# Gate tables from three bf16 products with the token as the last index, and value products in pairs of units

## The chip, the cores and the metric

The kernel runs on one core of a Trainium2 chip. The metric is the device time of one execution in microseconds; lower is better. TensorE (PE in the profile; PEld is its weight load), VectorE (DVE), ScalarE (ACT), GpSimd (POOL) and the DMA queue of SyncE (SP) work side by side and wait for one another through semaphores.

## What is computed

The reference chains two transformer blocks over 512 tokens of width 1024. The last part of the second block is a PEER feed-forward layer. For each token and each of 8 heads it picks 16 of 128 x 128 experts, and uses them with softmax weights:

```python
experts = jnp.take_along_axis(cand_i, best_pos, axis=-1)
g = jax.nn.softmax(best_s, axis=-1)
act = jax.nn.gelu(jnp.einsum('thkd,td->thk', expert_u[experts], xb).astype(jnp.float32))
wgt = (g * act).astype(xb.dtype)
return jnp.einsum('thk,thkd->td', wgt, expert_v[experts])
```

All inputs and the output are float32. The first block's second layer is a forgetting attention with 16 heads (8 pairs) over 4 query tiles of 128 tokens.

## The kernel before

The work is one long program of stages: even mixer, feed-forward, odd mixer (`odd`), feed-forward, the second block's mixer (`second`), and `peer`. Big products are made in three float32r matmuls of split operands (`mm3`, L181 to L183). Each engine runs its instructions in a fixed order.

**Gate tables in `peer`.** For the first 384 tokens (three tiles of 128) the kernel doesn't gather experts: it multiplies all 16384 experts densely and weighs them with a table G of 128 x 128 gates for each token. A token has 128 picks (8 heads x 16), which lie on the partitions: `idx[0]` and `idx[1]` hold the two index halves of each pick, `idx[2]` its gate. `flush` (L1582) turns a tile's three fields to that layout with PE transposes and ACT copies (L1588). `peer_pair` (L1652) then makes, for a block of `TB` = 16 tokens, two one-hot tables `oB` and `Ag` of 128 picks x (16 tokens x 128 keys) in float32, by two `is_equal` on DVE (L1659); it multiplies `Ag` with the gate, 8 tokens in one DVE instruction (L1662) and 8 tokens each in an ACT instruction (L1664). `peer_g` (L1667) makes one float32 matmul for each token, `oB[:, token]` as weights and `Ag[:, token]` as moving operand (L1675), four tokens into a PSUM bank; ACT copies the bank to `st` with the token as last index (L1676), and SP writes `st` to `Gd` in DRAM (L1677).

The order is written out in the loop over the 24 blocks: `peer_g` of a block, `peer_pair` of the next, then one `u_block` (two in every third turn), then two indirect gathers of experts for the last tile of tokens, which GpSimd issues and DVE uses. A `u_block` is 24 float32r matmuls of 128 x 384 (L181 to L183) on a panel of `peer_u`, which is loaded by SP, split by ACT (L170) and DVE (L175). There are 24 + 8 = 32 of them in this loop.

**Attention in `odd`.** `attend` (L501) runs over 32 units, a pair of heads p and a query tile i in order. In step u it issues some matmuls of projection panels, the scores of unit u (L480, L481, L1036) with their softmax on DVE and ACT, the value products of unit u-2 (L1046), and the transposes of unit u-1 (L496 in `p_t`), whose results go to buffers `PT`, three of them. A value product has 64 columns of weights and writes one half of the PSUM partitions, so the two heads of a pair stand side by side in the array.

Of the kernel before, what the change touches and what calls it, by code (L numbers as in the profile page):

```python
# [10 lines left out]
F32 = mybir.dt.float32  # L11
F32R = mybir.dt.float32r
BF16 = mybir.dt.bfloat16
U32 = mybir.dt.uint32
I32 = mybir.dt.int32
AF = mybir.ActivationFunctionType
ALU = mybir.AluOpType
# [4 lines left out]
P = 128  # L22
D = 1024
T = 512
# [9 lines left out]
NKEY = 128  # L34
TB = 16
TD = T - P
# [14 lines left out]
class Builder:  # L51
    def __init__(self, nc, tc, ctx, ins, out, plan=None):
        self.nc, self.tc, self.ctx, self.I, self.out = nc, tc, ctx, ins, out
        ec = ctx.enter_context
        self.cp = ec(tc.tile_pool(name="cp", bufs=1))
        self.wp = ec(tc.tile_pool(name="wp", bufs=4))
        self.big = ec(tc.tile_pool(name="big", bufs=3))
        self.np_ = ec(tc.tile_pool(name="np", bufs=2))
        self.flip = 0
        self.qs_bufs = 3  # L60
        self.lo_pool = False
        self.nx = self.nst = self.last_evac = None
        self.npre = 0
        self.log, self.plan, self.pos, self.ready, self.look = [], plan, 0, [], 2
        self.x = self.cp.tile([P, NT, D], F32, name="x")
        for t in range(NT):
            nc.sync.dma_start(self.x[:, t], ins["x"][t * P:(t + 1) * P])
        self.idn = self.cp.tile([P, P], F32, name="idn")
        nc.sync.dma_start(self.idn, ins["idn"])
        self.idb = self.cp.tile([P, P], BF16, name="idb")  # L70
        nc.vector.tensor_copy(self.idb, self.idn)
        self.gcols = self.cp.tile([P, 6, KD], F32, name="gcols")
        nc.sync.dma_start(self.gcols, ins["gcols"])
        self.ones = self.cp.tile([P, P], F32, name="ones")
        nc.vector.memset(self.ones, 1.0)
        self.adacol = self.cp.tile([P, 6, KD], F32, name="adacol")
        self.adabc = self.cp.tile([P, 6, KD], F32, name="adabc")
        nc.sync.dma_start(self.adabc, ins["adab_col"])
        self.sc = self.cp.tile([P, 2, KD], F32, name="sc")
        nc.sync.dma_start(self.sc, ins["cc"])  # L80
# [408 lines left out]
            nc.vector.tensor_mul(rs, rs, gate)  # L489
        nc.vector.tensor_scalar(Pm[:, :n], Pm[:, :n], rs, None, op0=ALU.mult)  # L490

    def p_t(self, wk, Pm, nb, tag="PT", bufs=3):
        nc = self.nc
        tp = self.tt_()
        for b in range(nb):
            nc.tensor.transpose(tp[:, b * P:(b + 1) * P], Pm[:, b * P:(b + 1) * P], self.idn)  # L496
        PT = wk.tile([P, T], F32, name=tag, tag=tag, bufs=bufs)
        self.copy(PT[:, :nb * P], tp[:, :nb * P])
        return PT

    def attend(self, wk, units, score, nb, value, panels, want, finish):  # L501


        done, Pm, PT = 0, {}, {}
        left = {}
        for u in units:
            left[u[0]] = left.get(u[0], 0) + 1
        for u in range(len(units) + 2):
            for _ in range(want(u) - done):
                next(panels, None)  # L510
                done += 1
            if u < len(units):
                sms = [wk.tile([P, 1], F32, name="sm", bufs=6) for _ in range(2)]
                Pm[u] = [score(*units[u], e, sms[e]) for e in range(2)]
                for e in range(2):
                    self.norm_p(wk, Pm[u][e], nb(units[u][1]) * P, sms[e])
            if u >= 2:
                p = units[u - 2][0]
                value(*units[u - 2], PT.pop(u - 2))
                left[p] -= 1  # L520
                if left[p] == 0:
                    finish(p)
            if 0 <= u - 1 < len(units):
                PT[u - 1] = [self.p_t(wk, q, nb(units[u - 1][1])) for q in Pm.pop(u - 1)]
        for _ in panels:
            pass
# [421 lines left out]

    def odd(self):
        nc, tc, I = self.nc, self.tc, self.I  # L950
        self.qs_bufs = 2
        h = self.norm_t()
        with ExitStack() as cx:
            ap = cx.enter_context(tc.tile_pool(name="odp", bufs=1))
            wk = cx.enter_context(tc.tile_pool(name="odw", bufs=2))
# [7 lines left out]
            of = self.big.tile([P, KD, T], F32, name="of", tag="big")  # L963
# [12 lines left out]
            ps = self.ot_()  # L976
# [22 lines left out]
                nc.sync.dma_start(c6, I["one6"][0:1].broadcast_to([P, 8 * T]))  # L999
                nc.sync.dma_start(c6[0:3] if q else c6[3:6], I["one6"][1:2].broadcast_to([3, 8 * T]))  # L1000
            for i in range(3):
                pc = wk.tile([P, T], BF16, name="pc", tag="PT", bufs=3)[0:16]
                nc.vector.tensor_copy(pc, cum)
                if i < 2:
                    nc.vector.tensor_sub(cum, cum, pc)
                ng = wk.tile([P, T], BF16, name="ng", tag="PT", bufs=3)[0:16]
                nc.vector.tensor_scalar(ng, pc, -1.0, None, op0=ALU.mult)
                nc.sync.dma_start(cd[0, i], pc)
                nc.sync.dma_start(cd[1, i], ng)
# [3 lines left out]
            QK, po = {}, {}  # L1013
# [37 lines left out]
            def fill():  # L1051
# [3 lines left out]
                for k in range(6):  # L1055
# [4 lines left out]
            units = [(p, i) for p in range(8) for i in range(NT)]  # L1060
            self.attend(wk, units, score, lambda i: i + 1, value, fill(),
                        lambda u: min(128, 4 * u + 20) + max(0, 2 * u - 56),
                        lambda p: self.copy(of[:, p], po[p]))
            self.sqrt_table(self.last_exp)
            self.split_k(oT, of, (6, 7))
            w3 = ap.tile([P, 4, D], F32R, name="w3", tag="cq6", bufs=1)
# [75 lines left out]
    def second(self):  # L1142
        nc, tc, I = self.nc, self.tc, self.I
        self.qs_bufs = 2
        with ExitStack() as c0:
            p0 = c0.enter_context(tc.tile_pool(name="s2p", bufs=1))
            uT = p0.tile([P, 4, T], F32, name="uT", tag="uT", bufs=1)
            h = self.norm_t()
            with ExitStack() as cx:
                ap = cx.enter_context(tc.tile_pool(name="s2a", bufs=1))  # L1150
                dp = cx.enter_context(tc.tile_pool(name="s2d", bufs=1, space=DRAM))
                wk = cx.enter_context(tc.tile_pool(name="s2w", bufs=2))
# [11 lines left out]
                for q in range(2):  # L1164
                    ps = self.mmt()
# [22 lines left out]
            with ExitStack() as cx:  # L1188
                ap = cx.enter_context(tc.tile_pool(name="s2g", bufs=1))
                wk = cx.enter_context(tc.tile_pool(name="s2n", bufs=2))  # L1190
# [24 lines left out]
                for c in range(4):  # L1215
                    ps = self.ot_()
# [100 lines left out]
    def peer(self):  # L1317
        nc, tc, I = self.nc, self.tc, self.I
        self.look = 0
        with ExitStack() as c0:  # L1320
# [16 lines left out]
                nc.scalar.copy(h2t[:, c * T:(c + 1) * T], tp)  # L1337
            gk = ExitStack()
            ep = gk.enter_context(tc.tile_pool(name="pee", bufs=2))
            idx = [ep.tile([P, TD], F32, name=f"ix{q}", bufs=1) for q in range(3)]  # L1340
            it128 = ep.tile([P, NKEY], F32, name="it128", bufs=1)
            nc.sync.dma_start(it128, I["iota"].broadcast_to([P, NKEY]))
            eid = ap.tile([P, P], I32, name="eid")
            g3 = ap.tile([P, P], F32, name="g3")
            act3 = ap.tile([P, P], F32, name="act3")
# [79 lines left out]
                        next(gs)  # L1425
                        ng -= 1
            gp = gk.enter_context(tc.tile_pool(name="peg", bufs=2))
            behind[0], pair = self.peer_pair(gp, idx, it128, 0)
            for tb in range(NTB):
                self.peer_g(gp, pair, tb, Gd)  # L1430
                if tb + 1 < NTB:
                    behind[0], pair = self.peer_pair(gp, idx, it128, tb + 1)
                if tb == 4:
                    next(steps, None)
                u_block()
                if tb % 3 == 2:
                    u_block()
                for _ in range(2 if tb < NTB - GSTOP else 0):
                    next(gs, None)
# [102 lines left out]
    def peer_topk(self, wk, h, idx, it128, eid, g3, ep):  # L1542
# [39 lines left out]
        def flush():  # L1582
            t, ef = wait
            tp = self.tt_()
            for q in range(3):
                nc.tensor.transpose(tp[:, q * P:(q + 1) * P], ef[q], self.idn)
            for q in range(3):
                nc.scalar.copy(idx[q][:, t * P:(t + 1) * P], tp[:, q * P:(q + 1) * P])  # L1588

        for t in (3, 0, 1, 2):  # L1590
            c = wk.tile([P, 8, NC_], F32, name="cand")
# [60 lines left out]
    def peer_pair(self, wk, idx, it, tb):  # L1652

        nc = self.nc
        ia, ib, g = [q[:, tb * TB:(tb + 1) * TB] for q in idx]
        oB = wk.tile([P, TB, NKEY], F32, name="oB")
        Ag = wk.tile([P, TB, NKEY], F32, name="Ag")
        for o, ix in ((oB, ib), (Ag, ia)):
            nc.vector.tensor_tensor(o, it.unsqueeze(1).broadcast_to([P, TB, NKEY]),  # L1659
                                    ix.unsqueeze(2).broadcast_to([P, TB, NKEY]), op=ALU.is_equal)  # L1660
        n = TB // 2
        last = nc.vector.tensor_tensor(Ag[:, 0:n], Ag[:, 0:n], g[:, 0:n].unsqueeze(2).broadcast_to([P, n, NKEY]), op=ALU.mult)  # L1662
        for t in range(n, TB):
            nc.scalar.activation(Ag[:, t], Ag[:, t], AF.Copy, scale=g[:, t:t + 1])  # L1664
        return last, (oB, Ag)

    def peer_g(self, wk, pair, tb, Gd):  # L1667

        nc = self.nc
        oB, Ag = pair  # L1670
        st = wk.tile([P, NKEY, TB], F32, name="gst")
        for q in range(TB // 4):
            ps = self.tt_() if q % 2 else self.st_()
            for t in range(4):
                nc.tensor.matmul(ps[:, t * P:(t + 1) * P], oB[:, q * 4 + t], Ag[:, q * 4 + t], start=True, stop=True)  # L1675
            nc.scalar.copy(st[:, :, q * 4:q * 4 + 4].rearrange("p i t -> p t i"), ps.rearrange("p (t i) -> p t i", t=4))  # L1676
        nc.sync.dma_start(Gd[tb], st)  # L1677

# [181 lines left out]
```

## Time and profile before

| | us |
|---|---|
| median of 3 runs | 3028.69 (3024.31 to 3030.38) |
| profiled execution, its own time | 3035.33 |
| span of the profiled execution | 3033.6 |
| PE busy | 2983.7 (98%) |
| DVE busy | 2153.1 (71%) |
| ACT busy | 1394.7 (46%) |
| stretch of the gate tables, about 1990 to 2215 | 225 |
| stretch of the attention in `odd`, about 812 to 984 | 172 |

Matmuls are pipelined and the ends of their records are modelled, so PE's cost is read from the distances between starts in the timeline, not from the durations. Lines are those of the kernel before.

### The profile page before, as it was taken

How to read it: one execution, taken by the hardware profiler on the slowest of the kernel's cores; microseconds unless marked ns; L12 is line 12 of the kernel's file. 1: busy time of each engine (PE TensorE's matmuls, PEld its weight loads, DVE VectorE, ACT ScalarE, POOL GpSimd, SP SyncE). 2: the span in 40 equal slices, each digit the busy share in tenths (PEclk: the TensorE clock that was granted, in tenths of full speed). 3: DMA queues.
4: the chain of work that ended last, by engine and by line, in shares of the span. 5: the costliest groups of instructions: out<-in, count | busy, mean ns of one | idle time of the engine just before them, and what ended most of it. 6: DMA issues, size and time to landing. Idle time of an engine off the chain costs nothing.

```text
span 3033.6 us, 42326 instructions
## 1 busy us (share of the span) xinstructions
PE 2983.7 (98%) x15672; PEld 2526.6 (83%) x15672; DVE 2153.1 (71%) x3994; ACT 1394.7 (46%) x2374; POOL 638.3 (21%) x661
## 2 busy tenths in 40 slices
PE   8999999999999999999999999999999999999998
PEld 6867787788777878888888889999988888888887
DVE  3378798745577655556853689979947777777777
ACT  4466532224455443445662344568743333333333
POOL 2400000000000000000000100146625555555451
PEclk9999999999999999999999999999999999999999
DMA  4210367624311355554332326889899989999884
GB/s 130 84 36 22 95 192 223 193 83 135 101 49 41 118 182 193 193 188 140 104 98 91 110 79 200 282 297 323 309 319 309 339 310 337 311 331 319 316 307 162
DMA packets 212262, 580.19 MB, mean 191 GB/s; under 512 B 19372, under 2 KB 86092, under 8 KB 208588
## 3 DMA queue, kind: packets, MB, share of 16 engines
q1 hardware_dynamic: 167128, 414.95, 41.3%
q0 software_dynamic: 44352, 161.50, 14.8%
q8 instruction: 123, 2.02, 0.3%
q10 hardware_dynamic: 576, 1.05, 0.1%
q14 instruction: 83, 0.68, 0.1%
HBM read 522.80 MB, written 54.62 MB: 190 GB/s over the span
## 4 chain that ended last, share of the span: by engine, by line
PE 77%; DVE 10%; DMA 4%; ACT 3%; issue 1%; DVEq 0%; SPq 0%; ACTq 0%
PE mm L182 10%; PE mm L181 10%; PE mm L183 10%; PE acc L182 5%; PE acc L183 5%; PE acc L181 5%; PE mx L181 4%; PE mx L182 4%; PE mx L183 4%; PE tp L496 2%; PE tp L182 1%; PE tp L181 1%; PE tp L183 1%; PE sc L182 1%; PE sc L183 1%; PE sc L181 1%
## 5 line engine op out<-in xcount | busy, mean ns | idle before, releaser
L170 ACT CAST wh<-raw 128x1024 fp32r<-128x1024 f32 x476 | 500.6, 1052 | 1029.8 <-PE mm L182 405.7
L175 DVE TENSOR_TENSOR wl<-raw,wh 128x1024 fp32r<-128x1024 f32 x432 | 531.2, 1232 | 451.4 <-ACT wh L170 444.7
L181 PE MATMUL mm<-bh,wh 128*128 128x384 f32 (+2 forms) x1680 | 606.1, 361 | 0.2 <-ACT act L1359 0.2
L183 PE MATMUL mm<-bh,wl 128*128 128x384 f32 (+2 forms) x1680 | 602.0, 358 | 1.3 <-DVE wl L175 1.2
L182 PE MATMUL mm<-bl,wh 128*128 128x384 f32 (+2 forms) x1680 | 602.2, 358 | 0.0
L183 PEld LDWEIGHTS mm<-bh,wl 128*128 128x128 f32 x1680 | 315.6, 188 | 32.2 <-DVE wl L175 2.3
L181 PEld LDWEIGHTS mm<-bh,wh 128*128 128x128 f32 x1680 | 315.8, 188 | 31.7 <-ACT act L1359 0.4
L182 PEld LDWEIGHTS mm<-bl,wh 128*128 128x128 f32 x1680 | 315.9, 188 | 31.0 <-issue 0.3
L181 PE MATMUL acc<-wh,wth 128*128 128x512 f32 x768 | 300.8, 392 | 7.4 <-ACT wth L1487 4.8
L182 PE MATMUL acc<-wl,wth 128*128 128x512 f32 x768 | 301.8, 393 | 1.0 <-DVE wl L175 1.0
L183 PE MATMUL acc<-wh,wtl 128*128 128x512 f32 x768 | 301.9, 393 | 0.0
L181 PE MATMUL mx<-bh,wh 128*128 128x512 f32 (+2 forms) x584 | 216.3, 370 | 0.0
L183 PE MATMUL mx<-bh,wl 128*128 128x512 f32 (+2 forms) x584 | 213.6, 366 | 0.4 <-DVE wl L175 0.4
L182 PE MATMUL mx<-bl,wh 128*128 128x512 f32 (+2 forms) x584 | 213.9, 366 | 0.0
L181 PEld LDWEIGHTS acc<-wh,wth 128*128 128x128 f32 x768 | 145.1, 189 | 38.1 <-ACT wth L1487 5.9
L183 PEld LDWEIGHTS acc<-wh,wtl 128*128 128x128 f32 x768 | 145.3, 189 | 31.3 <-DVE wtl L1489 0.9
L182 PEld LDWEIGHTS acc<-wl,wth 128*128 128x128 f32 x768 | 145.2, 189 | 30.7 <-DVE wl L175 1.5
L140 POOL DMA_DIRECT2D pre<-in_peer_u x2 | 1.3, 664 | 657.5 <-DVE bl L285 657.5
L183 PEld LDWEIGHTS mx<-bh,wl 128*128 128x128 f32 x584 | 109.9, 188 | 15.0 <-DVE wl L175 0.7
L181 PEld LDWEIGHTS mx<-bh,wh 128*128 128x128 f32 x584 | 109.9, 188 | 14.3 <-issue 0.5
L182 PEld LDWEIGHTS mx<-bl,wh 128*128 128x128 f32 x584 | 109.9, 188 | 14.2 <-issue 0.5
L1375 POOL DMA_INDIRECT gat<-in_peer_ut,eid x64 | 104.4, 1631 | 18.8 <-issue 11.7
(605 smaller groups left out, 6077.1 us busy)
## 6 DMA issues: line engine op xcount, KB each, us to landing
raw<-in_peer_u SPq DMA_DIRECT2D x128, 512.0 KB
raw<-in_peer_v SPq DMA_DIRECT2D x128, 512.0 KB
raw<-in_ffn_wi SPq DMA_DIRECT2D x88, 512.0 KB
araw<-in_ada_w SPq DMA_DIRECT2D x48, 512.0 KB
Gd<-gst SPq DMA_DIRECT2D x24, 1024.0 KB
G<-Gd SPq DMA_DIRECT2D x16, 1536.0 KB
raw<-in_ffn_wo SPq DMA_DIRECT2D x44, 512.0 KB
raw<-in_w2A SPq DMA_DIRECT2D x32, 512.0 KB
```

The source lines that it names most:

```text
L140: nc.gpsimd.dma_start(b[:, i], u[i])
L170: nc.scalar.copy(wh, raw)
L175: (nc.gpsimd if on_pool else nc.vector).tensor_sub(wl, raw, wh)
L181: nc.tensor.matmul(out, ah, bh, start=first, stop=False)
L182: nc.tensor.matmul(out, ah, bl, start=False, stop=False)
L183: nc.tensor.matmul(out, al, bh, start=False, stop=last)
L496: nc.tensor.transpose(tp[:, b * P:(b + 1) * P], Pm[:, b * P:(b + 1) * P], self.idn)
L1375: nc.gpsimd.indirect_dma_start(out=r, out_offset=None, in_=table, in_offset=bass.IndirectOffsetOnAxis(ap=eid[:, hk:hk + 1], axis=0))
```

## The change

In `peer`: the gate is written as a sum of three bf16 numbers (`idx[2]`, `idx[3]`, and the rest in `idx[4]`, which is float32). `oB`, `Ag`, the index fields and the row of key numbers (`itr`, copied to 16 tokens) become bf16, and the tables' free layout turns from (token, key) to (key, token), so that the last index has 16 contiguous elements of 2 bytes. `Ag` holds three tables, one for each part of the gate. `peer_pair` has two `is_equal`, two full multiplications and a half one on DVE, and the same 8 activations on ACT. `peer_g` has three bf16 matmuls for each token, accumulated in PSUM; their weights and moving operands step by 16 elements, which is 32 bytes. `it128` moves to a buffer of another pool, and is copied to `itr` once.

In `odd`: value products come in every second step, two units at a time (`burst=2`), with six `PT` buffers.

```diff
-    def p_t(self, wk, Pm, nb, tag="PT", bufs=3):
+    def p_t(self, wk, Pm, nb, tag="PT", bufs=None):
...
-        PT = wk.tile([P, T], F32, name=tag, tag=tag, bufs=bufs)
+        PT = wk.tile([P, T], F32, name=tag, tag=tag, bufs=bufs or self.ptb)
...
-            if u >= 2:
-                p = units[u - 2][0]
-                value(*units[u - 2], PT.pop(u - 2))
+            for w in range(u - 1 - burst, u - 1) if u >= 2 and (u - 1) % burst == 0 else ():
+                p = units[w][0]
+                value(*units[w], PT.pop(w))
...
     def odd(self):
...
+        self.ptb = 6
...
-                        lambda p: self.copy(of[:, p], po[p]))
+                        lambda p: self.copy(of[:, p], po[p]), burst=2)
...
-            idx = [ep.tile([P, TD], F32, name=f"ix{q}", bufs=1) for q in range(3)]
-            it128 = ep.tile([P, NKEY], F32, name="it128", bufs=1)
+            idx = [ep.tile([P, TD], F32 if q == 4 else BF16, name=f"ix{q}", bufs=1) for q in range(5)]
+            it128 = wk.tile([P, D], F32, name="it128", tag="gat", bufs=4)[:, 0:NKEY]
             nc.sync.dma_start(it128, I["iota"].broadcast_to([P, NKEY]))
+            itr = ep.tile([P, NKEY, TB], BF16, name="itr", bufs=1)
+            nc.vector.tensor_copy(itr, it128.unsqueeze(2).broadcast_to([P, NKEY, TB]))
...
+            ts = slice(t * P, (t + 1) * P)
             for q in range(3):
-                nc.scalar.copy(idx[q][:, t * P:(t + 1) * P], tp[:, q * P:(q + 1) * P])
+                nc.scalar.copy(idx[q][:, ts], tp[:, q * P:(q + 1) * P])
+            rest = ep.tile([P, P], F32, name="grest", bufs=1)
+            nc.vector.tensor_sub(rest, tp[:, 2 * P:3 * P], idx[2][:, ts])
+            nc.scalar.copy(idx[3][:, ts], rest)
+            nc.vector.tensor_sub(idx[4][:, ts], rest, idx[3][:, ts])
...
     def peer_pair(self, wk, idx, it, tb):
...
-        ia, ib, g = [q[:, tb * TB:(tb + 1) * TB] for q in idx]
-        oB = wk.tile([P, TB, NKEY], F32, name="oB")
-        Ag = wk.tile([P, TB, NKEY], F32, name="Ag")
-        for o, ix in ((oB, ib), (Ag, ia)):
-            nc.vector.tensor_tensor(o, it.unsqueeze(1).broadcast_to([P, TB, NKEY]),
-                                    ix.unsqueeze(2).broadcast_to([P, TB, NKEY]), op=ALU.is_equal)
+        ia, ib, g1, g2, g3 = [q[:, tb * TB:(tb + 1) * TB] for q in idx]
+        rows = lambda q: q.unsqueeze(1).broadcast_to([P, NKEY, q.shape[-1]])
+        oB = wk.tile([P, NKEY, TB], BF16, name="oB")
+        Ag = wk.tile([P, 3, NKEY, TB], BF16, name="Ag")
+        nc.vector.tensor_tensor(oB, it, rows(ib), op=ALU.is_equal)
+        A = Ag[:, 2]
+        nc.vector.tensor_tensor(A, it, rows(ia), op=ALU.is_equal)
         n = TB // 2
-        last = nc.vector.tensor_tensor(Ag[:, 0:n], Ag[:, 0:n], g[:, 0:n].unsqueeze(2).broadcast_to([P, n, NKEY]), op=ALU.mult)
+        nc.vector.tensor_tensor(Ag[:, 0], A, rows(g1), op=ALU.mult)
+        nc.vector.tensor_tensor(Ag[:, 1], A, rows(g2), op=ALU.mult)
+        last = nc.vector.tensor_tensor(A[:, :, 0:n], A[:, :, 0:n], rows(g3[:, 0:n]), op=ALU.mult)
         for t in range(n, TB):
-            nc.scalar.activation(Ag[:, t], Ag[:, t], AF.Copy, scale=g[:, t:t + 1])
+            nc.scalar.activation(A[:, :, t], A[:, :, t], AF.Copy, scale=g3[:, t:t + 1])
         return last, (oB, Ag)
...
     def peer_g(self, wk, pair, tb, Gd):
...
-                nc.tensor.matmul(ps[:, t * P:(t + 1) * P], oB[:, q * 4 + t], Ag[:, q * 4 + t], start=True, stop=True)
+                for e in range(3):
+                    nc.tensor.matmul(ps[:, t * P:(t + 1) * P], oB[:, :, q * 4 + t], Ag[:, e, :, q * 4 + t], start=e == 0,
+                                     stop=e == 2)
```

## Rows read from the trace of the kernel before

**Rows 1.** Chain that ended last, by engine, from the page.
```profile
PE 77%; DVE 10%; DMA 4%; ACT 3%; issue 1%; DVEq 0%; SPq 0%; ACTq 0%
```

**Rows 2.** Busy time by stretch: length, each engine's busy time, PEclk, DMA share, GB/s.
```profile
812.00:984.00 172.00, 171.50 (x1056) 130.74 (x1056) 127.61 (x362) 100.18 (x235) 0.00 (x0) 1.00 0.15 47
...
1990.00:2215.00 225.00, 223.24 (x1553) 221.68 (x1552) 205.83 (x181) 182.79 (x343) 126.52 (x84) 1.00 0.87 315
...
2245.00:2260.00 15.00, 11.45 (x47) 8.90 (x46) 8.50 (x15) 4.08 (x6) 7.26 (x7) 0.93 1.06 376
```

**Rows 3.** Timeline of PE in the gate stretch: start, duration, line, names, shape, count.
```profile
2049.09 0.33 PE L182 MATMUL mm<-bl,wh 128*128 128x384 f32 x1
2049.26 0.33 PE L183 MATMUL mm<-bh,wl 128*128 128x384 f32 x1
2049.43 1.05 PE L1675 MATMUL sc<-Ag,oB 128*128 128x128 f32 x8
2050.32 1.06 PE L1675 MATMUL tp<-Ag,oB 128*128 128x128 f32 x8
```

**Rows 4.** Groups by line and shape, 1990 to 2215: count, busy us, mean ns.
```profile
L1664 ACT ACTIVATE Ag<-Ag,ix 128x128 f32<-128x128 f32 x176 | 60.9, 411 | 15.5 <-DVE Ag L1659 15.5
...
L1676 ACT COPY gst<-sc 128x512 f32<-128x512 f32 x48 | 52.0, 1084 | 0.0
L1675 PE MATMUL tp<-Ag,oB 128*128 128x128 f32 x384 | 51.1, 276 | 0.1
...
L1659 DVE TENSOR_TENSOR oB<-it,ix 128x2048 f32<-128x2048 f32 x22 | 50.3, 2285 | 1.4 <-PE tp L1675 1.4
...
L1662 DVE TENSOR_TENSOR Ag<-Ag,ix 128x1024 f32<-128x1024 f32 x22 | 26.8, 1217 | 0.0
```

**Rows 5.** Timeline of PE around three runs of 64-column products in halves of the array.
```profile
135.02 1.10 PE L622 MATMUL tp<-pe,wc 128*64 128x1 f32 x32
136.05 0.50 PE L181 MATMUL sc<-bh,wh 128*128 128x512 f32 x1
...
139.68 2.04 PE L617 MATMUL ob<-KC,wc 128*64 128x64 f32 x32
141.66 0.50 PE L181 MATMUL sc<-bh,wh 128*128 128x512 f32 x1
...
836.42 1.09 PE L1046 MATMUL ob<-PT,v 128*64 128x128 f32 x16
837.45 0.44 PE L496 MATMUL tp<-idn,Sm 128*128 128x128 f32 x2
```

**Rows 6.** Timeline of PE at one bf16 product of 128 columns.
```profile
96.14 0.23 PE L845 MATMUL mm<-mst,idb 128*128 128x128 bf16 x1
96.18 0.36 PE L842 MATMUL mm<-Ks,Qs 128*128 128x256 f32 x1
```

**Rows 7.** Groups by line: two bf16 instructions of DVE in the top-16 selection.
```profile
L1633 DVE TENSOR_TENSOR peq<-peq,tib 128x2048 bf16<-128x2048 bf16 x8 | 9.7, 1216 | 0.0
L1631 DVE TENSOR_TENSOR peq<-ra__16465,it 128x2048 bf16<-128x2048 bf16 x1 | 2.3, 2284 | 0.0
```

**Rows 8.** Groups by line: ACT copies of a whole PSUM bank into contiguous rows.
```profile
L116 ACT COPY PT<-tp 128x512 f32<-128x512 f32 x32 | 18.8, 586 | 14.7 <-PE tp L496 9.7 <-issue 4.9
```

**Rows 9.** Timeline of PE in the attention of `odd`: two steps, without and with value products.
```profile
815.64 0.28 PE L1036 MATMUL sc<-cs,cq 128*128 128x256 bf16 x1
815.95 0.33 PE L496 MATMUL tp<-idn,Sm 128*128 128x128 f32 x1
...
841.36 0.34 PE L1036 MATMUL sc<-cs,cq 128*128 128x384 bf16 x1
841.62 0.44 PE L1046 MATMUL ob<-PT,v 128*64 128x128 f32 x4
841.99 0.66 PE L496 MATMUL tp<-idn,Sm 128*128 128x128 f32 x4
```

**Rows 10.** Timeline of PE at the start of `peer`, in brackets its wait.
```profile
1755.03 0.41 PE L299 MATMUL tp<-idn,xn 128*128 128x128 f32 x2 [0.43 <-DVE xn L361]
```

More of the change, by code (lines that the diff above doesn't have):

```diff
@@ L62, in __init__ @@
         self.nx = self.nst = self.last_evac = None
-        self.npre = 0
+        self.npre, self.ptb = 0, 3
         self.log, self.plan, self.pos, self.ready, self.look = [], plan, 0, [], 2
@@ L496, in p_t, with attend @@
             nc.tensor.transpose(tp[:, b * P:(b + 1) * P], Pm[:, b * P:(b + 1) * P], self.idn)
-        PT = wk.tile([P, T], F32, name=tag, tag=tag, bufs=bufs)
+        PT = wk.tile([P, T], F32, name=tag, tag=tag, bufs=bufs or self.ptb)
         self.copy(PT[:, :nb * P], tp[:, :nb * P])
         return PT
-    def attend(self, wk, units, score, nb, value, panels, want, finish):
+    def attend(self, wk, units, score, nb, value, panels, want, finish, burst=1):
         done, Pm, PT = 0, {}, {}
@@ L1001, in odd @@
             for i in range(3):
-                pc = wk.tile([P, T], BF16, name="pc", tag="PT", bufs=3)[0:16]
+                pc = wk.tile([P, T], BF16, name="pc", tag="PT", bufs=self.ptb)[0:16]
                 nc.vector.tensor_copy(pc, cum)
@@ L1005, in odd @@
                     nc.vector.tensor_sub(cum, cum, pc)
-                ng = wk.tile([P, T], BF16, name="ng", tag="PT", bufs=3)[0:16]
+                ng = wk.tile([P, T], BF16, name="ng", tag="PT", bufs=self.ptb)[0:16]
                 nc.vector.tensor_scalar(ng, pc, -1.0, None, op0=ALU.mult)
@@ L1144, in second @@
         self.qs_bufs = 2
+        self.ptb = 3
         with ExitStack() as c0:
@@ L1427, in peer @@
             gp = gk.enter_context(tc.tile_pool(name="peg", bufs=2))
-            behind[0], pair = self.peer_pair(gp, idx, it128, 0)
+            behind[0], pair = self.peer_pair(gp, idx, itr, 0)
             for tb in range(NTB):
@@ L1431, in peer @@
                 if tb + 1 < NTB:
-                    behind[0], pair = self.peer_pair(gp, idx, it128, tb + 1)
+                    behind[0], pair = self.peer_pair(gp, idx, itr, tb + 1)
                 if tb == 4:
```

## Prediction

> **What bounds the kernel now.** I read the chain that ended last first: 77% of it is PE, so time is won or lost where PE's own work grows or shrinks [rows 1]. Then the busy time by stretch, for the two stretches that the diff touches [rows 2]. In the gate stretch PE is busy 223.24 of 225 us, DVE 205.83 and ACT 182.79: PE sets the pace, but DVE has only 225 - 206 = 19 us of slack. In the attention of `odd` PE is busy 171.5 of 172 us. PE's clock is at its upper level (1.00 granted) in both. Behind the gate stretch, at 2245 to 2260, PE is busy 11.45 of 15 us with the DMA engines full (1.06): a hole of 3.55 us. The sum is made on the profiled execution, 3035.33 us, which is 0.2% above the median of 3028.69; the result is scaled by 3028.69/3035.33.
>
> **PE in the gate stretch, taken out.** A float32 product of a token is two records of 128 x 128. In the timeline eight records, four tokens, take 2050.32 - 2049.43 = 0.89 us [rows 3], so 222 ns a token and 111 ns a record. 24 blocks of 16 tokens make 384 tokens: 384 x 0.2225 = 85.4 us. (The group of one bank has x384 records [rows 4], its twin as many: 768 records for 384 tokens.)
>
> **PE in the gate stretch, put in: the disputed term.** Three bf16 products a token are 1152. Their price depends on operands that step by 32 bytes, and no row has a bf16 product like that, so it is bounded. Lower end: contiguous operands. A bf16 product of 128 columns lets the next matmul start after 0.04 us [rows 6]. The float32r products of 384 columns follow each other every 0.17 us [rows 3], so 128 columns at that rate are 57 ns; I take 56. Upper end: the one run of PE with a stepped moving operand. L617 reads `KC` with a step of 16 float32 (64 bytes), 64 columns; 32 records take 141.66 - 139.68 = 1.98 us, 62 ns each. L1046, the same 64-column weights in the same alternation of array halves but contiguous, takes 1.03 us for 16 records of 128 columns, 64 ns each [rows 5]. Half the columns cost the same, so a stepped column costs twice a contiguous one. Weights aren't the cause: L622 loads the same weights for one column each in 1.03 us for 32 records, 32 ns each. With two halves of the array at work, a record lasts about 2 x 55 = 110 ns once the 0.2 us at the ends is taken off, so a stepped column costs 110/64 = 1.72 ns, a contiguous one 110/128 = 0.86.
>
> ACT shows the same for stores: a copy of a bank into contiguous rows takes 586 ns [rows 8], into `st` with a step of 64 bytes 1084 ns [rows 4]. So 32 bytes may cost nothing (56 ns), twice the contiguous rate (2 x 56 = 112 ns), or the same time for each step as in L617 (128 x 1.72 = 220 ns). I take 112: both measured cases doubled. That is 1152 x 0.112 = 129.0 us, and **the gate stretch gets 129.0 - 85.4 = 43.6 us longer**. The break-even is 222.5/3 = 74 ns a product.
>
> [...]
>
> **DVE and ACT in the gate stretch.** Before, a block costs DVE 2 x 2285 + 1217 = 5787 ns [rows 4]. After: L1633 is the pattern of the new instructions (bf16, the second input repeated over a middle index with 16 contiguous elements) at 1216 ns; L1631, repeated along the last index, takes 2284 [rows 7]. Four such and the half multiplication with a float32 gate: 4 x 1216 + 1217 = 6081 ns, 24 x 0.294 = 7.1 us more: 212.9 us, hidden behind PE if PE gets slower, and the floor if it gets faster. If `is_equal` stays slow, 24 x 2 x 1.07 = 51 us more, 264 us, still just under PE's 223 + 44 = 267. ACT's 8 activations a block step by 32 bytes too: between 0 and (1084 - 586)/512 x 128 = 125 ns each, up to 24 us in all, 207 us: hidden behind PE either way. SP's queue has the same transfers in the same order.
>
> **Once only.** The copy to `itr` (2048 elements) costs DVE up to 2.3 us, as L1631 does. It falls where PE waits for DVE's norm [rows 10], so 0 to 2.3 us are exposed; I take 1. The three flushes each add two DVE instructions and one on ACT of 128 columns; ACT waits there for DVE with weight splits queued behind. PE has panels queued meanwhile; I take 0, and 1 us each as bound. The hole at 2245 comes from full DMA engines; a slower gate stretch spreads the same bytes: 0 to 3.5 us come back, I take 1.5.
>
> **Value products in pairs.** From the last score to the value products and on to the transposes takes 0.26 + 0.37 us [rows 9]. Streaming the last score (384 columns, 0.17) and two pairs of records (2 x 0.11) explains 0.39; about 0.24 are the two turns of the array. Pairing removes 16 of 32 such bursts. In return the scores turn to transposes directly: 0.31 us with 0.11 of streaming at 815.64, so 0.20 (its wait for the softmax may be in it). So 0.04 to 0.24 us are saved at each: 0.6 to 4 us, and I take 2.5. Who waits: in even steps the transposes of unit u-1 come 0.4 to 1.0 us sooner behind its softmax, and could wait for DVE; that would eat the gain. The six buffers hold the four waiting `PT` and two new ones, so nothing waits for a buffer.
>
> **Sum.** 43.6 + 1 - 1.5 - 2.5 = +40.6 us on 3035.3, 3075.9; scaled, 3069.2. I say **3069**, with 3050 to 3086 for this case (100 to 120 ns a product, the small terms at their ends).
>
> **The rivals.**
>
> Faster: 32 bytes cost PE nothing. Then PE needs 1152 x 0.056 = 64.5 us, 20.9 less, but DVE's 212.9 us become the bound, with ACT's 207 close behind: of 225 at most 12 us go, and I take 9, as neither will run without gaps. With -2.5 and +1 that is -10.5 us, 3018 (3010 to 3025). It decides below 74 ns. For it: 32 bytes are nearer than 64, and the element is half as wide. Against: both stepped cases doubled. [...]
>
> Much slower: the price is a fixed 1.72 ns for each step, whatever the element, or stepped weights are loaded in line with the products (112 + 112). Then 1152 x 0.22 = 253 us, +168: about 3196. For it: ACT's step costs (1084 - 586)/512 = 0.97 ns on top of its own 0.83, 1.8 in all, close to PE's 1.72 though the engines differ. Against: L617's two halves together read a step every 0.86 ns.
>
> In between: a price around 74 ns, no change.
>
> **Chances.** Forecast 0.50, faster 0.27, much slower 0.16, in between 0.07. Some 0.2% (6 us) is what a measurement can tell from no change. The faster case reaches below 3022.6 in nearly all of its range: faster 0.25; same 0.09; slower 0.66. The range from 3012 to 3086 holds the forecast, the faster case and the one between, and leaves out the much slower one.
>
> **What would show it.** Distances between starts of L1675's successor: 112 ns, against 56 or 220; the length of the gate stretch, about 268 us against 213 or 390; DVE's `is_equal` at 1216 ns; ACT's activations up to 0.13 us longer; PE's clock unchanged; the attention of `odd` 2 to 3 us shorter. Wrong would be: contiguous speed at 32 bytes, or a chain that runs through DVE in the gate stretch.

## The result and the profile after

The changed kernel takes 3245.19 us (median of 5 runs, 3242.11 to 3249.86) against 3028.69 us: ratio 1.0715, 95% interval 1.0703 to 1.0726. Its profiled execution took 3242.11 us, with a span of 3240.3. Where a kernel below has one time and no interval, it was executed once.

First the page of the kernel after: PE's busy share and granted clock in 40 slices of 81 us, and the chain that ended last.

```profile
PE   8999999999999999999999999999999999999998
...
PEclk9999999999999999999999998777769999999999
...
PE 80%; DVE 8%; DMA 4%; ACT 2%; issue 1%; DVEq 0%; ACTq 0%; SPq 0%
```

PE is still the bound, a little more than before [rows 1]. New is the clock: it is down in six slices, and these hold the gate stretch. Next the busy times by stretch of the kernel after (length, then PE, PEld, DVE, ACT, POOL, PEclk, DMA share, GB/s): the attention of `odd`, 100 us of the gate stretch, the part behind it, and then one turn of the gate loop in small pieces.

```profile
812.00:984.00 172.00, 170.47 (x1082) 132.72 (x1082) 131.31 (x366) 103.14 (x237) 0.00 (x0) 1.00 0.16 54
...
2100.00:2200.00 100.00, 100.00 (x432) 76.57 (x431) 50.99 (x58) 56.36 (x79) 16.85 (x23) 0.73 0.45 154
...
2440.00:2500.00 60.00, 58.65 (x290) 51.89 (x289) 40.26 (x59) 22.34 (x32) 22.82 (x27) 1.00 0.95 318
...
2098.00:2104.80 6.80, 6.80 (x41) 6.71 (x39) 5.61 (x8) 4.63 (x8) 0.00 (x0) 1.00 0.69 228
2104.90:2110.60 5.70, 5.70 (x25) 3.61 (x25) 1.26 (x2) 2.55 (x3) 2.20 (x4) 0.78 0.55 174
2110.70:2116.20 5.50, 5.50 (x25) 3.40 (x24) 0.00 (x0) 2.12 (x2) 0.00 (x0) 0.50 0.37 138
2116.30:2121.40 5.10, 5.10 (x18) 5.10 (x17) 4.77 (x7) 4.77 (x9) 0.00 (x0) 0.50 0.50 206
2121.80:2123.00 1.20, 1.20 (x8) 1.05 (x7) 1.20 (x2) 0.70 (x2) 0.00 (x0) 1.00 0.00 0
```

In the gate stretch PE is busy 100 of 100 us, DVE only 51 and ACT 56: before, DVE was at 206 of 225 [rows 2]. Nothing but PE holds this stretch. The small pieces show the clock: 1.00 before the products, falling during them to 0.50, still 0.50 in the 5 us of float32r matmuls behind them, then 1.00 again. The same turn in PE's timeline (start, duration, line, names, shape, count):

```profile
2104.70 0.34 PE L183 MATMUL mm<-bh,wl 128*128 128x384 f32 x1
2104.88 3.10 PE L1689 MATMUL sc<-Ag,oB 128*128 128x128 bf16 x12
2107.79 3.06 PE L1689 MATMUL tp<-Ag,oB 128*128 128x128 bf16 x12
2110.67 3.06 PE L1689 MATMUL sc<-Ag,oB 128*128 128x128 bf16 x12
2113.54 3.05 PE L1689 MATMUL tp<-Ag,oB 128*128 128x128 bf16 x12
2116.23 0.69 PE L181 MATMUL mx<-bh,wh 128*128 128x384 f32 x1
2116.71 0.52 PE L182 MATMUL mx<-bl,wh 128*128 128x384 f32 x1
2117.03 0.52 PE L183 MATMUL mx<-bh,wl 128*128 128x384 f32 x1
...
2121.79 0.34 PE L183 MATMUL mx<-bh,wl 128*128 128x384 f32 x1
```

Four tokens, 12 products, take 2.87 to 2.91 us, so a product takes about 241 ns, where two float32 records took 222 a token [rows 3]. The distance is the same in the first bank (2104.88 to 2107.79, clock at 1.00 at its start) as in the third (2110.67 to 2113.54, clock 0.50): it isn't the clock that sets it. Over the whole stretch the median distance is 241 ns both for the 401 products that start at the upper clock and for the 727 at the lower one. The float32r matmuls behind do follow the clock, 0.32 us apart (2116.71 to 2117.03) for the 0.17 of [rows 3], until 2121.79.

The first and last product, of the kernel after and then of the kernel before (count, min/median/max ns, first and last start):

```profile
L1689 PE MATMUL sc<-Ag,oB x576: 411/423/455, 1994.9 to 2422.9; 128*128 128x128 bf16 x192
L1689 PE MATMUL tp<-Ag,oB x576: 411/423/428, 1997.8 to 2425.8; 128*128 128x128 bf16 x192
```

```profile
L1675 PE MATMUL sc<-Ag,oB x384: 272/275/377, 1994.3 to 2207.8; 128*128 128x128 f32 x192
L1675 PE MATMUL tp<-Ag,oB x384: 275/275/377, 1995.2 to 2208.7; 128*128 128x128 f32 x192
```

From first to last it is 430.9 us for 214.4, **216.5 us more**. That this is also the difference of the medians is partly chance: the attention is 4.2 us shorter, the time up to the first product some 3.4 us longer (both below). The stretch has two parts, by the distances between PE's starts: the products hold PE 24 x (2116.23 - 2104.88) = 272 us for 85, **+187**; the 720 float32r matmuls of the u_blocks hold it 157.8 us for 128.8 (all their distances summed in each trace), **+29**.

The groups of the kernel after from 2000 to 2400 (count, busy us, mean ns, idle before and its releaser):

```profile
L1677 ACT ACTIVATE Ag<-Ag,ix 128x128 bf16<-128x128 bf16 x168 | 103.7, 1041 | 0.0
...
L1691 ACT COPY gst<-sc 128x512 f32<-128x512 f32 x43 | 45.9, 1068 | 73.5 <-PE sc L1689 50.2 <-issue 23.1 <-ACT act L1363 0.2
...
L1669 DVE TENSOR_TENSOR oB<-itr,ix 128x2048 bf16<-128x2048 bf16 x22 | 26.9, 1225 | 164.9 <-PE tp L1689 164.9
```

`is_equal` takes 1225 ns for 2285 [rows 4], and DVE then stands idle 164.9 us for PE to free the tables. An activation costs ACT 103.7/168 = 617 ns of busy time for 60.9/176 = 346 [rows 4].

Last the attention of `odd` in the kernel after, two steps in PE's timeline, and the second of these steps in the kernel before:

```profile
841.01 0.34 PE L1037 MATMUL sc<-cs,cq 128*128 128x384 bf16 x1
841.18 0.60 PE L496 MATMUL tp<-idn,Sm 128*128 128x128 f32 x4
...
845.54 0.39 PE L1037 MATMUL sc<-cs,cq 128*128 128x512 bf16 x1
845.86 0.88 PE L1047 MATMUL ob<-PT,v 128*64 128x128 f32 x12
846.66 0.88 PE L496 MATMUL tp<-idn,Sm 128*128 128x128 f32 x6
```

```profile
846.42 0.39 PE L1036 MATMUL sc<-cs,cq 128*128 128x512 bf16 x1
846.74 0.66 PE L1046 MATMUL ob<-PT,v 128*64 128x128 f32 x8
847.33 0.88 PE L496 MATMUL tp<-idn,Sm 128*128 128x128 f32 x6
```

From the last score to the transposes the two steps took 0.63 us [rows 9] and 0.91 before; now 0.17 and 1.12. That is 0.25 us less for this pair of steps. Other pairs differ, so the stage as a whole decides: from its first score to its last value products it takes 164.6 us (815.38 to 980.02) for 168.9 (815.64 to 984.49), **4.2 us less**, or 0.26 us for each of 16 pairs.

### The profile page after: what moved, and what is told of

Its sections match the earlier page's. It is cut to its first block, busy times and chain, and to the rows that moved or that the text cites. A ratio compares the mean times of both kernels' runs of the same rounds, so it can differ in the third digit from the quotient of the medians.

```text
span 3240.3 us, 43122 instructions
## 1 busy us (share of the span) xinstructions
PE 3193.1 (99%) x16056; PEld 2636.3 (81%) x16056; DVE 2161.3 (67%) x4049; ACT 1469.8 (45%) x2377; POOL 582.0 (18%) x661
## 4 chain that ended last, share of the span: by engine, by line
PE 80%; DVE 8%; DMA 4%; ACT 2%; issue 1%; DVEq 0%; ACTq 0%; SPq 0%
PE mm L182 10%; PE mm L181 10%; PE mm L183 10%; PE acc L182 5%; PE acc L183 5%; PE acc L181 5%; PE sc L1689 4%; PE tp L1689 4%; PE mx L181 4%; PE mx L182 4%; PE mx L183 4%; PE tp L496 1%; DMA raw<-in_ffn_wo 1%; PE tp L182 1%; PE tp L183 1%; PE tp L181 1%
## 5 line engine op out<-in xcount | busy, mean ns | idle before, releaser
L181 PE MATMUL mm<-bh,wh 128*128 128x384 f32 (+2 forms) x1680 | 617.0, 367 | 1.6 <-ACT act L1363 1.0
L182 PE MATMUL mm<-bl,wh 128*128 128x384 f32 (+2 forms) x1680 | 610.5, 363 | 0.0
L183 PE MATMUL mm<-bh,wl 128*128 128x384 f32 (+2 forms) x1680 | 609.5, 363 | 0.7 <-DVE wl L175 0.7
L181 PEld LDWEIGHTS mm<-bh,wh 128*128 128x128 f32 x1680 | 323.5, 193 | 34.6 <-ACT act L1363 1.3
L182 PEld LDWEIGHTS mm<-bl,wh 128*128 128x128 f32 x1680 | 322.8, 192 | 30.9 <-issue 0.3
L1689 PEld LDWEIGHTS <-oB 128*128 128x128 bf16 x1152 | 169.1, 149 | 104.0 <-issue 2.7
L1689 PE MATMUL sc<-Ag,oB 128*128 128x128 bf16 x576 | 149.3, 424 | 0.0
L1689 PE MATMUL tp<-Ag,oB 128*128 128x128 bf16 x576 | 148.4, 422 | 0.0
L1669 DVE TENSOR_TENSOR oB<-itr,ix 128x2048 bf16<-128x2048 bf16 x24 | 29.4, 1224 | 164.9 <-PE tp L1689 164.9
```

The source lines that it names most:

```text
L181: nc.tensor.matmul(out, ah, bh, start=first, stop=False)
L182: nc.tensor.matmul(out, ah, bl, start=False, stop=False)
L183: nc.tensor.matmul(out, al, bh, start=False, stop=last)
L1669: nc.vector.tensor_tensor(oB, it, rows(ib), op=ALU.is_equal)
L1689: nc.tensor.matmul(ps[:, t * P:(t + 1) * P], oB[:, :, q * 4 + t], Ag[:, e, :, q * 4 + t], start=e == 0, stop=e == 2)
```

## Experiments

Theory at the start: PE pays for the moving operand by the 16 bytes of SBUF that its columns touch, whatever the clock; the 16 bytes are an assumption, which the groups of 8, 4 and 2 tokens test. Rivals: any step costs the same; the weights' step costs too; the clock is the cause, and not a result.

**The value pairs alone** (the kernel before, with `burst=2` and six `PT` buffers).

```diff
-        self.npre = 0
+        self.npre, self.ptb = 0, 3
...
+            for w in range(u - 1 - burst, u - 1) if u >= 2 and (u - 1) % burst == 0 else ():
```

> The kernel before with the value products in pairs and the six PT buffers alone; gate tables as before. In the trace of the changed kernel the last value products of the odd attention start 4.2 us earlier than before (980.02 against 984.49, of which 0.3 us were there at its first score), and the keys of the peer stage 2.95 us earlier. Theory that the pairing gains this: the stretch of the attention is 3 to 5 us shorter and the whole 3 to 4 us, 3025 us, ratio 0.9988. Rival, that the gain is eaten behind the stage: same as before within 1 us.

Measured: 3023.34 us against 3027.84, ratio 0.9986 (0.9977 to 0.9995). The gain of about 4 us is real, and it is nearly all that the change gains; the gate tables alone then cost 3245 - 3023 = 222 us.

This run also explains a difference that is none of the change's. Behind the gate stretch the trace of after is shorter than that of before. The same 40 us of that part, first of the kernel before, then of the one with the pairs alone, whose code there is the same:

```profile
2860.00:2900.00 40.00, 36.32 (x169) 31.31 (x168) 27.01 (x30) 13.19 (x18) 15.48 (x20) 0.96 0.82 286
```

```profile
2860.00:2900.00 40.00, 40.00 (x195) 35.31 (x194) 30.86 (x34) 15.18 (x20) 17.56 (x20) 1.00 0.92 319
```

The profiled execution of before lost time there that the same code doesn't lose here. From its first product with `peer_v` to its last it takes 786.4 us, the one with the pairs alone 775.9 and the one of after 774.6. Its 3035.33 us were 6.6 above its median, those of after 3.1 below theirs, and so the two spans differ by 206.7 us and the medians by 216.5.

**Groups of 8, 4 and 2 tokens.** All tables as `[P, TB // G, NKEY, G]`, so that the operands step by 16, 8 or 4 bytes in place of 32 (`GW` and `GM` are G for the weights and the moving operand, here equal).

```diff
-        oB = wk.tile([P, NKEY, TB], BF16, name="oB")
-        Ag = wk.tile([P, 3, NKEY, TB], BF16, name="Ag")
+        oB = wk.tile([P, TB // GW, NKEY, GW], BF16, name="oB")
+        Ag = wk.tile([P, 3, TB // GM, NKEY, GM], BF16, name="Ag")
...
+                    nc.tensor.matmul(ps[:, t * P:(t + 1) * P], oB[:, (q * 4 + t) // GW, :, (q * 4 + t) % GW],
+                                     Ag[:, e, (q * 4 + t) // GM, :, (q * 4 + t) % GM], start=e == 0, stop=e == 2)
```

> Tables with 8 tokens last: every operand of the gate products steps by 16 bytes, one element for each 16 bytes. So far: a moving operand at 32 bytes takes 232 to 241 ns, at 8 bytes 118. Theory A, the price is 1.8 ns for each 16 bytes that are touched: 16 bytes cost as much as 32, 230 to 241 ns, granted clock near 0.72, 3235 to 3250 us. Theory S, the price grows with the step: between 118 and 241, about 160 to 190 ns, 3125 to 3190 us.

> The changed kernel with the token last in groups of 4 only: tables are (4 groups, 128 keys, 4 tokens), so the products step by 8 bytes in place of 32 and two elements of a product lie within 16 bytes. Theory A, a step pays when it goes to another 16 bytes each time: a product takes 55 to 75 ns, PE leaves the bound, DVE's 213 us set the gate stretch, granted clock 1.00, 3010 to 3030 us. Theory A2, two elements for one price: about 120 ns a product, 1152 x 0.12 - 85 = +53, and 3070 to 3090 us. Theory B, every step costs 1.8 ns whatever its size: 241 ns a product, clock near 0.72, 3235 to 3250 us.

> Tables with 2 tokens last: a step of 4 bytes, four elements for each 16 bytes. Theory A: 4 columns for 1.8 ns is 58 ns a product, level with contiguous ones, 1152 x 0.060 = 69 us against 85.4; if DVE keeps its 1.22 us an instruction with 2 elements in its innermost run, DVE's 213 us and ACT's 165 to 170 set the stretch, 210 to 215 us against 214, and with 4.4 us from the pairs 3015 to 3025 us, ratio 0.997. If DVE loses its rate (2285 ns): 24 x (4 x 2285 + 1217) + 67 = 315 us, 3110 to 3125 us. Theory S (any step costs): over 74 ns a product.

PE's timeline, two banks of 12 products each; first groups of 8:

```profile
2104.70 2.99 PE L1703 MATMUL sc<-Ag,oB 128*128 128x128 bf16 x12
2107.52 2.98 PE L1703 MATMUL tp<-Ag,oB 128*128 128x128 bf16 x12
```

Groups of 4:

```profile
2104.69 1.59 PE L1703 MATMUL tp<-Ag,oB 128*128 128x128 bf16 x12
2106.10 1.59 PE L1703 MATMUL sc<-Ag,oB 128*128 128x128 bf16 x12
```

Groups of 2:

```profile
2112.98 0.85 PE L1703 MATMUL tp<-Ag,oB 128*128 128x128 bf16 x12
2113.67 0.85 PE L1703 MATMUL sc<-Ag,oB 128*128 128x128 bf16 x12
```

A product takes 2.82/12 = 235 ns, 1.41/12 = 118 and 0.69/12 = 57. So 32 and 16 bytes cost nearly the same (241 and 235), and from 16 to 8 to 4 bytes the price halves each time that twice as many columns fit into 16 bytes. It is 128 x 16 bytes touched in 235 ns, 64 in 118, 32 in 57: 1.8 ns for each. At 4 bytes this can't be told from the price of no step at all: a contiguous moving operand has eight columns in 16 bytes, and its products are no cheaper (62 ns, in the next experiment). That is theory A at 16 and 4 bytes, and A2 at 8; that every step costs the same falls, and so does a price that grows from 16 to 32 bytes as it did up to 16. L617, at 64 bytes, had 1.72, an estimate of the prediction from [rows 5]. For the bf16 products here two columns in 16 bytes weren't enough for the contiguous price (118 ns), and four were (57).

The times: 3238.73 us for groups of 8; 3075.41 for groups of 4 (1.0161, 1.0145 to 1.0176), with a granted clock of 0.99 from 2000 to 2200; 3046.84 for groups of 2 (1.0058, 1.0041 to 1.0074). With 57 ns the products need less of PE than the float32 ones did, and still the kernel is slower than before; the last experiments ask why.

**One operand stepped at a time**, by `GW, GM = 16, 1` and `GW, GM = 1, 16`.

> Only the weights step: oB stays with 16 tokens last (32-byte step), the three Ag tables are bf16 with each token contiguous. Theory M, the moving operand is the cost (L617 of before had a stepped moving operand alone): products 56 to 75 ns apart, clock 1.00; DVE becomes the bound, since its repeated gate is along the last index again (24 x (1216 + 3 x 2284 + 1217) = 223 us and 67 us of other work, 290 us against 225), about 3095 us. Theory W, stepped weights are loaded in line at the same price: products 110 to 241 ns apart, 3120 to 3245 us.

> Only the moving operand steps: the Ag tables stay with 16 tokens last (32-byte step), oB is bf16 with each token contiguous. Theory M: products about 241 ns apart as in the changed kernel, clock near 0.72 in the gate stretch, 3235 to 3250 us. Theory W: products 56 to 130 ns apart, under 3110 us. If 220 ns, the 1.72 ns a step of L617 is the moving operand's price and some 20 ns come from the weights.

PE's timeline with the weights alone stepped (10 products, then the next), and a group of DVE from 1990 to 2215 of the same kernel:

```profile
2100.38 0.79 PE L1703 MATMUL sc<-Ag,oB 128*128 128x128 bf16 x10
2101.00 1.41 PE L1703 MATMUL tp<-Ag,oB 128*128 128x128 bf16 x20
```

```profile
L1679 DVE TENSOR_TENSOR Ag<-itr,ix 128x2048 bf16<-128x2048 bf16 x15 | 60.6, 4041 | 0.0
```

PE's timeline with the moving operand alone stepped:

```profile
2107.08 2.96 PE L1703 MATMUL tp<-Ag,oB 128*128 128x128 bf16 x12
2109.87 2.96 PE L1703 MATMUL sc<-Ag,oB 128*128 128x128 bf16 x12
```

Weights: 0.62/10 = 62 ns, which is also the median of all these products at the upper clock. The 68 that start at the lower clock are 107 ns apart, so contiguous columns follow the clock where the stepped ones above don't. Moving operand: 2.79/12 = 232 ns, 3247.31 us, granted clock 0.71 from 2000 to 2200. So theory M holds: the moving operand makes the price, and the weights add at most 241 - 232 = 9 ns. The kernel with stepped weights took 3140.19 us, 45 more than I expected: DVE is its bound, as foreseen (busy 199 of 200 us from 2000 to 2200, PE 154), but one `is_equal` a block, with single elements 32 bytes apart in one input and the other repeated along the last index, takes 4041 ns where I had put 2284; 24 x 1.76 us are 42 of the 45.

**Short runs of products**, six float32r matmuls of a u_block behind each bank.

```diff
+                part = u_parts()
-                self.peer_g(gp, pair, tb, Gd)
+                self.peer_g(gp, pair, tb, Gd, lambda: next(part, None))
```

> The changed kernel, 32-byte step, with the order on PE changed: six of a u_block's 24 float32r matmuls behind each 12 gate products, in place of 24 behind 48. In the changed kernel 48 products run for 11.6 us, then the granted clock is at its lower level for some 5 us of float32r matmuls, spaced 320 ns for 173; over the stretch that is 157.8 us for 720 of them against 129.0 in the kernel before, 28.8 us. Theory R, the clock answers to the long run of stepped products: with short runs it stays up, products still at 241 ns, 3245 - 29 = about 3216 us. Theory P, it answers to the share of stepped products whatever their order: lower for some or all of the stretch, between 3216 and 3320 us (all 720 matmuls at 320 ns: +77 us on 3245).

PE's timeline of this kernel:

```profile
2109.91 3.07 PE L1705 MATMUL sc<-Ag,oB 128*128 128x128 bf16 x12
2112.62 0.65 PE L181 MATMUL mx<-bh,wh 128*128 128x384 f32 x1
2113.07 0.52 PE L182 MATMUL mx<-bl,wh 128*128 128x384 f32 x1
2113.39 0.52 PE L183 MATMUL mx<-bh,wl 128*128 128x384 f32 x1
```

3276.48 us, 31 more than the changed kernel. Theory R falls, and the time lies in P's range of 3216 to 3320: behind this run of only 12 products the float32r matmuls are 0.32 us apart too. The mean granted clock is a little higher, 0.76 from 1995 to 2459 against 0.71 in the changed kernel's stretch, but more of the float32r matmuls meet the lower level: between the first product and the last 325 of 738 start at it, against 207 of 720. By the distances between starts the float32r matmuls hold PE 206 us there, for 158, and the products 256, for 273. There are also more turns between the two kinds, at 0.45 us from 2112.62 to 2113.07 in place of 0.32. The order doesn't rescue the clock here. With groups of 4, at 118 ns a product, it was 0.99, and with the moving operand alone stepped 0.71: the 29 us come with the slow products. No run has a stretch of slow products that keeps the upper clock, so whether any order would keep it up stays open; the products themselves cost 241 ns at either level. Slow products aren't the only way to lose it: in two kernels in which PE waits, the mean from 2000 to 2200 was 0.94 (groups of 2) and 0.88 (the weights alone stepped).

**Why 57 ns a product gain nothing.** With groups of 2, PE's own work in the stretch is less than before, but the stretch takes 1995.6 to 2228.5, 233 us, for 214. The waits from 1990 to 2230, of all engines and then of SP's queue (line, waited for: us, times, longest):

```profile
ACT wh L172 <- DMA raw<-in_peer_u: 37.5, 11, 7.6
PE mm L183 <- ACT wh L172: 19.6, 4, 8.7
```

```profile
SPq L1706 <- ACT Ag L1691: 72.7, 14, 12.2
```

The same wait of SP's queue with the value pairs alone, whose tables are float32:

```profile
SPq L1679 <- ACT Ag L1666: 39.8, 15, 4.5
```

PE waits for the split of the next panel, ACT for its load, and SP's queue stands at L1706, the store of `gst`, waiting for ACT; the load is queued behind it. Another store makes SP's queue wait longer in all, that of `act` (L1371, 89.1 us), but with the value pairs alone it is 87.7 already, so it isn't what is new. Three edits ask whether this order or DVE's work is the floor. The first moves the store to ACT's queue:

```diff
-        nc.sync.dma_start(Gd[tb], st)
+        nc.scalar.dma_start(Gd[tb], st)
```

> Tables with 2 tokens last (products 57 ns apart, gate stretch 233 us against 214 in the kernel before), and the store of the gate table to Gd issued from ACT's queue in place of SP's. With 2 tokens last PE waits 24 us for the split of the next panel, ACT there waits 36.5 us for the panel's load, and SP's load stands behind a Gd store that waits for ACT's copies (72.7 us of waiting). Theory Q, the order on SP's queue is what eats the 18 us that the products gain: loads go out earlier, stretch 214 to 220 us, 3028 to 3034 us. Theory D, DVE is the floor (5.5 table instructions at 1.14 us a block, with its other work 216 us and more) and the late loads only follow from it: within 5 us of 3047.

The second keeps two bf16 numbers of the gate (some 16 bits):

```diff
-                for e in range(3):
+                for e in range(2):
...
-        nc.vector.tensor_tensor(Ag[:, 1], A, rows(g2, GM), op=ALU.mult)
```

> Tables with 2 tokens last and the gate as a sum of two bf16 numbers (some 16 bits) in place of three: two tables and two products for each token, so one full multiplication less a block on DVE (24 x 1.14 = 27 us) and 384 x 0.057 = 22 us less on PE. Theory D (DVE's floor): the stretch goes from 233 to 205 to 212 us, 3019 to 3026 us. Theory Q (SP's queue): at most 5 to 10 us go, 3037 to 3042.

> Both edits: two bf16 numbers a gate, and the Gd store on ACT's queue. If both theories hold a part, this is the fastest of the three: stretch 195 to 205 us, 3009 to 3020 us, below the kernel with the value pairs alone (3023). If only Q holds it is level with the kernel that has the store on ACT's queue alone; if only D, with the one of two numbers.

With the store on ACT's queue: 3026.7 us (0.9987, 0.9976 to 0.9997), 20 less than with the store on SP's. Its stretch from the first product to the last as a row of busy times, and the wait for the load:

```profile
1993.00:2211.00 218.00, 204.34 (x1878) 194.65 (x1878) 205.64 (x223) 179.75 (x335) 106.82 (x84) 0.98 0.86 308
```

```profile
ACT wh L172 <- DMA raw<-in_peer_u: 9.6, 6, 3.8
```

So theory Q holds for the lost 20 us: the store at the head of SP's queue delayed the loads. What is left, 218 us for 214, has DVE at 205.64 and PE at 204.34: the faster products put PE and DVE side by side, and neither runs without gaps. With two numbers a gate it is 3033.96 us (1.0015, 1.0005 to 1.0024), 13 less than with three, between the two theories. With both edits it is 3049.17 (1.0066, 1.0048 to 1.0084), against every expectation. There DVE waits 40.6 us for ACT's split and PE's weight loads 25.3 us at 78 issues; what causes it stays open.

No kernel with bf16 tables is shown to be faster than the one with the value pairs alone. Against the kernel before, each measured beside it, the pairs alone are at 0.9986 (0.9977 to 0.9995) and the best with bf16 tables, which has the pairs too, at 0.9987 (0.9976 to 0.9997): level, so the tables themselves gain nothing that these runs can tell.

## Why the prediction was wrong

**The step that failed** is the disputed term. Each of its three prices has a measured one near it, but only the highest at the step in question: 56 ns was measured as 57 (at 4 bytes), 112 as 118 (at 8), 220 as 241 (at 32, so 9% above what I had as the upper end). The choice among them was wrong. "I take 112: both measured cases doubled" made a factor out of a time. L617 gave 1.72 ns for a step [rows 5]; that is twice a contiguous column of that float32 product, 0.86 (the float32 products of the gate stretch have 111/128 = 0.87 [rows 3]), but four times one at the bf16 rate, 57/128 = 0.45. A step costs 1.8 to 1.9 ns in bf16 and 1.72 in float32, so half as wide an element, which I put down in favour of 32 bytes, buys nothing. ACT's 1.8 ns a step (0.97 from [rows 4] and [rows 8], and 0.83 of its own; its copies of 512 and 384 columns in the kernel before, 587 and 479 ns in the median, show (587 - 479)/128 = 0.84) stood in the text as an argument for the rival that came true, at a chance of 0.16. By the measured price the term is 272 - 85 = +187, not +43.6.

**The term that was missing** is the clock: "PE's clock unchanged" was written with no row behind it. It fell to 0.71, and the u_blocks, which the change doesn't touch, got 29 us longer. The much slower rival, 3196, misses by 49: 187 - 168 = 19 for its price, 29 for the clock, the rest small.

**The rival with stepped weights in line** falls: 62 ns a product. **The faster rival** was wrong on both of its steps: 57 ns needs four columns in 16 bytes, and its gain of 9 us didn't come even then (0.9987 of the kernel before with the store moved, 0.9986 without any new tables). DVE as the floor was named, SP's queue was not.

**DVE** is right: 1225 ns a table instruction, hidden. **ACT**: 271 ns more for an activation, where I had bounded it at 125, from copies whose output alone steps [rows 4]. Here the input does too; whether that is the reason wasn't tried. The other steps tell more, in busy time for one activation: 56.3/88 = 640 ns at 16 bytes, 50.8/146 = 348 at 8 and 50.5/160 = 316 at 4, and 35.5/116 = 306 with contiguous bf16 (the weights alone stepped). So with two elements in 16 bytes ACT pays 14% more than contiguous, where PE pays twice (118 ns for 57). At 32 bytes it is hidden, ACT being busy 56 of 100 us.

**Once only**: I took 1 us. From 1860 to 1995 PE is busy 131.66 of 135 us where it was 134.53, 2.9 us more idle, and the first gate product starts 3.4 us later than in the kernel with the pairs alone (1994.9 and 1991.5); the waits there are of about 1 us each, for a split, a load and an activation. The copy to `itr` itself took 1.22 us and PE didn't wait for it, so what is left is the time around the flushes, which I put at nothing, with 3 us as bound. Which instruction there makes PE wait isn't shown.

**The hole** behind the stretch shrank from 3.55 us to 1.35 (58.65 of 60 us busy from 2440 to 2500), so 2.2 us came back where I took 1.5. But with the pairs alone, whose gate stretch isn't slower, it is 2.1 us already (82.92 of 85 busy from 2215 to 2300), so most of that isn't shown to come from spreading the bytes.

**Value pairs**: I took 2.5 us in a range of 0.6 to 4, and it is 4.2; that is 0.26 us for each of 16 pairs on the average, so the upper price, 0.24, was the nearer one.

## What to carry to other kernels

Carry the price of a step in nanoseconds from one operation to another, never as a factor on a contiguous rate: with the faster element the factor was larger here, four in bf16 (1.8 ns for 0.45) in place of two in float32 (1.72 for 0.86). Before a table is laid out for one engine, ask how many columns of TensorE's moving operand fall into 16 bytes: with one a product took 235 ns here, with two 118, with four 57; the weights could be stepped here (62 ns), the moving operand couldn't (232). And an engine that is made faster gains only what its neighbours and the order of the queues leave: at 57 ns a product the kernel was at 1.0058 of the one before, and at 0.9987 once the store had left SP's queue. See which transfer is queued behind which wait.

## What the runs showed of the hardware

- A bf16 product of 128 columns takes 57, 118, 235 and 241 ns when both operands step by 4, 8, 16 and 32 bytes; 62 ns with the weights alone at 32, 232 with the moving operand alone. The 241 ns are the same at both levels of the clock; contiguous columns take 62 and 107.
- In stretches of products at 232 to 241 ns, in which PE is busy 198 to 200 of 200 us, the granted clock falls from 1.00 to 0.50 (mean 0.71; 0.76 with runs of 12 products, PE busy 460 of 464 us); the float32r matmuls behind them run 0.32 us apart for 0.17 until it is back. At 118 ns it stayed at 0.99.
- DVE's `is_equal` of 2048 bf16 elements takes 4041 ns with one element out of 32 bytes in one input and the other repeated along the last index; 1217 to 1225 with 2, 4 or 16 elements in the last index of both.
- ACT's activation of 128 bf16 elements with input and output stepped by 32 bytes costs 617 ns of its time, 348 with steps of 8 bytes and 316 with 4, for 306 contiguous in bf16 and 346 in float32.
